# Down projection of a SwiGLU block by seven block products for eight, and four small changes of order

## The chip, the cores and the metric

The kernel runs on one core of a Trainium2 chip. The metric is the device time of one execution in microseconds (us); a time given for a kernel is the median of several executions. TensorE (PE) does the matmuls, VectorE (DVE), ScalarE (ACT) and GpSimd (POOL) the elementwise work, and SyncE (SP), ACT and POOL issue the transfers (DMAs).

## The reference

One decoder layer runs for a prompt of 512 tokens and for 8 samples of 8 tokens, 576 tokens T in all that share the weights. With D = 1024 and three residual blocks, each with an RMS norm before and after it:

```
x = x + post(Wout · [Mamba2-SSD heads, mLSTM heads](pre(x)))     # one input projection for both
x = x + post(CrossAttention(pre(x), memory keys and values))
x = x + post(Wdown · (silu(Wgate · pre(x)) * (Wup · pre(x))))    # SwiGLU
```

FFN_HIDDEN is 2816, which is 22 units of 128. All is float32, and the outputs are the tokens, the memory's keys and values and the new states of the recurrent heads.

## The kernel before

Features lie on the 128 partitions and tokens along the free dimension, so a weight tile of 128 x 128 is the loaded operand and a stretch of tokens is streamed. Float32 products are made from three matmuls in the type fp32r: each operand is split into a high part `hi` (a cast) and the rest `lo` (a subtraction), and hi·hi, hi·lo and lo·hi are summed in PSUM (helper `gemm`, L201 to L203). A weight unit is loaded by SP into `raw`, cast to `whi` by ACT (L181) and its low part `wlo` is made by DVE (L188), or by POOL with a DMA that adds the weight onto its negated high part (L185 and L186). Tokens are taken in halves of 256 and 320 (`HALVES`) or, in the last block, 288 and 288 (`E`).

In the SwiGLU block the gate and up products of hidden units 4 to 21 are computed by class `Pair`: for two units, two halves of the tokens and two halves of D it makes seven products of blocks instead of eight (a Strassen scheme in Winograd's form). A `Pair` loads two units (`raw`, `rawx`), forms sums and differences of weight blocks on DVE (`sums`, L1701 and L1702; `diffs`, L1709 and L1710), splits them again (`parts2`, `parts3`, `parts4`), and takes two low parts from POOL's adding DMAs (`low`, L1693 and L1694: ACT negates, the DMA adds; tiles `wacc` and half of `wlo`). Its products go through `mul` (L1742 to L1744), and `done` adds the parts that PSUM doesn't add by itself. The sums of the tokens' blocks are made once. A `Pair`'s `early` and `mid` and the last `Pair`'s `late` are interleaved, so that the next weights are prepared while the last are multiplied.

The gated values of a unit are split into `hh` and `hl`. The down projection takes the hidden units in three chunks of 8, 8 and 6 (`down_chunk`): for each of 8 output units and both token halves a plain `gemm` over the chunk, whose result is stored into (`ev_first`), and then added onto (`ev_add`, DVE L1831), the sum `f_ffn`. The third chunk ends in the last norm and the store of the tokens.

The order on each engine comes from the tile framework: instructions are issued in the order of the calls, unless `tc.issue_after(...)` ties one behind another; an engine runs its queue in order and waits at its head. A buffer with `bufs=2` or `3` is taken again when its last reader is done, and a PSUM bank in the same way.

Other places that the change touches: the first loads and casts (L299 to L312); the recurrent state's update `h` (POOL L725, PE `ps_hu` L728, DVE L729) beside the split of `wv`; the first mixer inputs `mixm_h` (ACT L1021) beside the copy `f_mix` (ACT L1015) that empties a PSUM bank; and the product `ps_xo` for output unit 3 of the cross-attention.

## Time and profile before

| what | value |
|---|---|
| median of 3 executions | 1112.0 us (1111.62 to 1112.33) |
| the profiled execution's own time | 1111.46 us |
| its span, first to last instruction | 1109.7 us |
| PE / DVE / ACT / POOL busy, share of the span | 99% / 64% / 53% / 19% |
| granted TensorE clock | 0.998 |
| chain that ended last: PE / DMA / DVE / ACT | 91% / 3% / 3% / 2% |

Shares are of the whole span; a matmul's own duration includes its pipeline, so the pace of PE is read from the starts of matmuls in a row, and lost time from the idle times before them. 1.8 us of the execution lie around the span.

### The profile page before, as it was taken

What the parts mean: (1) busy time and instruction counts of PE and PEld (TensorE: products, weight loads), DVE (VectorE), ACT (ScalarE), POOL (GpSimd) and SP (SyncE); (2) the same over time, 40 slices, a digit from 0 to 9 for tenths busy, and PEclk for the clock granted to TensorE, in tenths of its full rate; (3) what the DMA queues carried; (4) which work ended last, traced back from release to release, by engine and by line L of the source; (5) the groups of instructions that cost most, each with busy time, mean ns of one, the idle gap of its engine ahead of it and who ended that gap; (6) DMA issues with size and microseconds to landing.
All of it is one profiled execution on the core that took longest, in us unless ns stands there. A gap on an engine that the chain in (4) does not pass through costs nothing.

```text
span 1109.7 us, 21067 instructions
## 1 busy us (share of the span) xinstructions
PE 1095.9 (99%) x8424; PEld 1049.6 (95%) x8424; DVE 708.7 (64%) x1393; ACT 590.1 (53%) x1066; POOL 214.0 (19%) x289
## 2 busy tenths in 40 slices
PE   9999999999999999999999999999999999999997
PEld 8999888998999999999988889999999999999997
DVE  6996686558877774669554545776533665447555
ACT  6877523256654564647454445556434674246654
POOL 1443544213122111000244202101001110011000
PEclk9999999999999999999999999999999999999999
DMA  6775634334745358552567765735435674257532
GB/s 219 184 149 115 162 134 152 124 99 141 228 135 138 81 182 287 194 184 96 199 215 254 275 200 190 249 102 130 137 96 128 172 165 125 93 119 170 125 132 86
DMA packets 55078, 176.57 MB, mean 159 GB/s; under 512 B 6044, under 2 KB 10268, under 8 KB 54468
## 3 DMA queue, kind: packets, MB, share of 16 engines
q1 hardware_dynamic: 41156, 136.88, 37.0%
q0 software_dynamic: 13248, 37.23, 16.5%
q8 instruction: 66, 1.08, 0.4%
q10 hardware_dynamic: 576, 1.11, 0.3%
q14 instruction: 32, 0.26, 0.1%
HBM read 154.54 MB, written 20.65 MB: 158 GB/s over the span
## 4 chain that ended last, share of the span: by engine, by line
PE 91%; DMA 3%; DVE 3%; ACT 2%; issue 1%; SPq 0%; DVEq 0%; POOL 0%; POOLq 0%; ACTq 0%
PE ps_in L201 6%; PE ps_in L202 6%; PE ps_in L203 6%; PE ps_dn L201 4%; PE ps_dn L203 4%; PE ps_dn L202 4%; PE ps_o L201 3%; PE ps_o L203 3%; PE ps_o L202 3%; PE ps_g L1742 3%; PE ps_g L1743 3%; PE ps_g L1744 3%; PE ps_u L1742 3%; PE ps_u L1743 3%; PE ps_u L1744 3%; PE ps_v L777 2%
## 5 line engine op out<-in xcount | busy, mean ns | idle before, releaser
L181 ACT CAST whi<-raw 128x1024 fp32r<-128x1024 f32 x110 | 114.7, 1046 | 125.0 <-PE ps_in L202 28.6
L201 PE MATMUL ps_in<-uh,whi 128*128 128x320 f32 (+1 forms) x544 | 163.6, 301 | 0.0
L203 PE MATMUL ps_in<-uh,wlo 128*128 128x320 f32 (+1 forms) x544 | 163.3, 300 | 0.2 <-DVE wlo L188 0.2
L188 DVE TENSOR_TENSOR wlo<-raw,whi 128x1024 fp32r<-128x1024 f32 (+1 forms) x102 | 107.6, 1056 | 86.9 <-ACT whi L181 84.5
L202 PE MATMUL ps_in<-ul,whi 128*128 128x320 f32 (+1 forms) x544 | 162.6, 299 | 0.0
L201 PEld LDWEIGHTS ps_in<-uh,whi 128*128 128x128 f32 x544 | 103.1, 190 | 2.4 <-issue 1.7
L203 PEld LDWEIGHTS ps_in<-uh,wlo 128*128 128x128 f32 x544 | 103.0, 190 | 1.4 <-DVE wlo L188 0.4
L202 PEld LDWEIGHTS ps_in<-ul,whi 128*128 128x128 f32 x544 | 103.2, 190 | 0.6
L201 PE MATMUL ps_dn<-hh,whi 128*128 128x320 f32 (+1 forms) x280 | 82.6, 298 | 0.5 <-ACT whi L181 0.5
L203 PE MATMUL ps_dn<-hh,wlo 128*128 128x320 f32 (+1 forms) x280 | 81.9, 295 | 0.8 <-DVE wlo L188 0.8
L202 PE MATMUL ps_dn<-hl,whi 128*128 128x320 f32 (+1 forms) x280 | 82.1, 294 | 0.0
L203 PEld LDWEIGHTS ps_dn<-hh,wlo 128*128 128x128 f32 x280 | 52.7, 189 | 1.2 <-DVE wlo L188 1.2
L201 PEld LDWEIGHTS ps_dn<-hh,whi 128*128 128x128 f32 x280 | 52.2, 188 | 1.0 <-ACT whi L181 0.7
L202 PEld LDWEIGHTS ps_dn<-hl,whi 128*128 128x128 f32 x280 | 52.8, 188 | 0.0
L186 POOL DMA_DIRECT2D wlo<-win x32 | 27.8, 879 | 86.8 <-ACT wlo L185 78.6
L1742 PE MATMUL ps_u<-b,whi 128*128 128x288 f32 x144 | 42.5, 295 | 0.6 <-ACT ct L1774 0.6
L1743 PE MATMUL ps_u<-b,whi 128*128 128x288 f32 x144 | 42.5, 296 | 0.0
L1742 PE MATMUL ps_g<-b,whi 128*128 128x288 f32 x144 | 42.5, 295 | 0.0
L1743 PE MATMUL ps_g<-b,whi 128*128 128x288 f32 x144 | 42.5, 295 | 0.0
L1694 POOL DMA_DIRECT2D wacc<-wgate x9 | 7.8, 862 | 161.4 <-ACT wacc L1693 140.7
L201 PE MATMUL ps_o<-mixs_h,whi 128*128 128x320 f32 (+1 forms) x128 | 38.3, 299 | 0.5 <-ACT f_mix L1015 0.5
L203 PE MATMUL ps_xo<-qh,wlo 128*128 128x288 f32 x128 | 37.7, 296 | 0.7 <-DVE wlo L188 0.7
(728 smaller groups left out, 3665.2 us busy)
## 6 DMA issues: line engine op xcount, KB each, us to landing
raw<-win SPq DMA_DIRECT2D x35, 512.0 KB, 3.7
raw<-wout SPq DMA_DIRECT2D x17, 512.0 KB, 3.6
kva<-kc SPq DMA_DIRECT2D x16, 512.0 KB, 6.6
kva<-vc SPq DMA_DIRECT2D x16, 512.0 KB, 6.8
raw<-wdown SPq DMA_DIRECT2D x16, 512.0 KB, 3.6
raw<-wxq SPq DMA_DIRECT2D x13, 512.0 KB, 3.5
raw<-wgate SPq DMA_DIRECT2D x13, 512.0 KB, 3.7
raw<-wup SPq DMA_DIRECT2D x13, 512.0 KB, 4.9
```

The lines of the kernel that those rows point to most:

```text
L181: A.copy(hi[:, :n], raw[:, :n])
L186: G.dma_start(lo[:, a:b], src[:, a:b], accum_op=ALU.add)
L188: e.tensor_tensor(lo[:, a:b], raw[:, a:b], hi[:, a:b].bitcast(F32), op=ALU.subtract)
L201: mm(ps, wh, ah, start=i == 0, stop=False)
L202: mm(ps, wh, al, start=False, stop=False)
L203: m = mm(ps, wl, ah, start=False, stop=i == len(tiles) - 1)
L777: m = mm(o, ah, lo[:, j:j + 256], start=False, stop=k == KT - 1, skip_group_check=True)
L1694: G.dma_start(out, s.src[j, :, c], accum_op=ALU.add)
L1742: mm(ps, wh, b[0][:, k, :], start=start and k == 0, stop=False, skip_group_check=True)
L1743: mm(ps, wh, b[1][:, k, :], start=False, stop=False, skip_group_check=True)
L1744: m = mm(ps, wl, b[0][:, k, :], start=False, stop=k == 3, skip_group_check=True)
```

## The change

`Pair` becomes a base class `Seven` with two users: `Pair` for gate and up, and a new class `Down` for the down projection. The hidden units are now taken in four chunks: units 0 to 3 plainly, 4 to 9 and 10 to 15 by `Down`, and 16 to 21 plainly as before. A `Down` makes two output units for both token halves over six hidden units, three in each half of the inner dimension: 7 products of 3 blocks of three matmuls, 63 matmuls of 288 columns, where the plain way takes 72 of 256 and 320. Four `Down` make a chunk. Their weights are prepared as a `Pair`'s are, 768 columns wide instead of 1024, and their order in memory is changed on the host.

The products need sums of the hidden blocks. Class `Hidden` stores three of the four blocks of a pair of units (`put`) and makes four differences in place (`sums`, DVE) and one split, 1152 wide, where the fourth block had its split of 288. It takes more memory: a tile `te`, a longer slot for `u3h`, and a pool `rows` that is closed earlier and opened again as `rows2`. `run` interleaves `Pair`s and `Down`s: the gate pair 10, four `Down`, the up pair 10, pairs 12 and 14; then again from 16 with the next chunk. A `Pair`'s first negation (`wacc`) is tied behind the first cast `c1` of the step ahead (`behind`). The program has 984 matmuls for the down projection instead of 1056; those for gate and up stay.

The four small orders: `par`, a table of 150 columns, is loaded through POOL's queue instead of SP's, and the first cast of a weight is made by DVE; the split of the first `wv` weights comes behind the first addition onto `h`; the first three `mixm_h` come behind the last copy `htc` of `qk`; in `ps_xo` for unit 3 the matmuls with `wlo` of the first six blocks come behind the other matmuls of those (`late=6`).

```diff
-    def split(hi, lo, src, eng=None):
-        A.copy(hi, src)
+    def split(hi, lo, src, eng=None, cast=None):
+        (cast or A.copy)(hi, src)
...
             (wh, wl), ah, al = tiles[k], xh(k, t0, n), xl(k, t0, n)
             mm(ps, wh, ah, start=i == 0, stop=False)
             mm(ps, wh, al, start=False, stop=False)
-            m = mm(ps, wl, ah, start=False, stop=i == len(tiles) - 1)
+            for c in range(late) if i == late - 1 else [i] if i >= late else ():
+                m = mm(ps, tiles[order[c]][1], xh(order[c], t0, n), start=False, stop=c == len(tiles) - 1)
...
-    S.dma_start(par, I["par"])
+    G.dma_start(par, I["par"])
...
         if k % 2 == 0:
             S.dma_start(raws[1][:, c], I["win"][2][:, c])
-            split(wi[0][0][:, c], wi[0][1][:, c], raws[0][:, c])
+            split(wi[0][0][:, c], wi[0][1][:, c], raws[0][:, c], cast=V.tensor_copy if k == 0 else None)
         uhk = A.activation(uh[:, k, 0:T], xraw[:, k, :], AF.Copy, scale=PAR("g_pre", k))
         ulk = V.scalar_tensor_tensor(ul[:, k, :], xraw[:, k, :], PAR("g_pre", k), uh[:, k, 0:T].bitcast(F32),
                                      op0=ALU.mult, op1=ALU.subtract)
...
+    added = []
...
             for g in range(2):
                 ps = BP("ps_hu")
                 mm(ps, bm[:, g * P:(g + 1) * P], xst[:, g * 512:(g + 1) * 512], start=True, stop=True)
-                V.tensor_tensor(hn[:, 8 * g:8 * g + 8, :], hn[:, 8 * g:8 * g + 8, :],
-                                ps.rearrange("p (h k) -> p h k", h=8), op=ALU.add)
+                added.append(V.tensor_tensor(hn[:, 8 * g:8 * g + 8, :], hn[:, 8 * g:8 * g + 8, :],
+                                             ps.rearrange("p (h k) -> p h k", h=8), op=ALU.add))
...
     for h in range(4):
-        gemm_tok(I["wv"][h], U, UL, CHUNKS, v_evac(h), 1024)
+        with tc.issue_after(added[0].ins) if h == 0 else ExitStack():
+            units = [split_w(I["wv"][h][:, i, :], cut=1024) for i in range(2)]
+        gemm_tok(I["wv"][h], U, UL, CHUNKS, v_evac(h), units=units)
...
     for j in range(8):
         hm = qk[:, 4 * (j % 2) + j // 2, 0:TP]
-        with tc.issue_after(evs[0].ins) if j > 2 else ExitStack():
+        with tc.issue_after((evs[0] if j > 2 else htc).ins):
             A.activation(mixm_h[:, j, 0:TP], hm, AF.Copy, scale=ghalf[:, j:j + 1])
...
-            m = gemm(ps, [(*w, KT)], act(oh), act(ol), t0, n, k0, k1, [2, 3, 4, 5, 6, 7, 0, 1])
+            m = gemm(ps, [(*w, KT)], act(oh), act(ol), t0, n, k0, k1, [2, 3, 4, 5, 6, 7, 0, 1], 6 if j == 3 else 0)
...
+    class Seven:
+
+        behind = ()
+
+        def weights_of(s, src1, src2, side, low=(None, None)):
+            s.n, s.side, s.src1, s.src2, s.made = src1.shape[-1] // 2, side, src1, src2, low
+            s.LA, s.LB, s.all = slice(0, s.n), slice(s.n, 2 * s.n), slice(0, 2 * s.n)
             s.r1 = wp.tile([P, 1024], F32, name="raw", tag="raw", bufs=2)
-            S.dma_start(s.r1, s.src[j])
+            S.dma_start(s.r1[:, s.all], src1)
...
-            s.low(s.l1, s.r1, s.j)
-
-        def low(s, out, raw, j, c=slice(0, 1024)):
-
-            if ("gu"[s.up], j) in PRE:
-                G.dma_start(out, pre[:, PRE.index(("gu"[s.up], j)), c])
+            with ExitStack() as after:
+                for t_ in s.behind:
+                    after.enter_context(tc.issue_after(t_.ins))
+                s.low(s.l1[:, s.all], s.r1[:, s.all], s.src1, s.made[0])
+
+        def low(s, out, raw, src, made):
+
+            if made is not None:
+                G.dma_start(out, made)
             else:
                 A.activation(out, raw, AF.Copy, scale=-1.0)
...
+
             fh, fl = s.factor(w)
-            for k in range(4):
+            nk = s.n // P
+            for k in range(nk):
                 wh, wl = fh[:, k, :], fl[:, k, :]
-                mm(ps, wh, b[0][:, k, :], start=start and k == 0, stop=False, skip_group_check=True)
-                mm(ps, wh, b[1][:, k, :], start=False, stop=False, skip_group_check=True)
-                m = mm(ps, wl, b[0][:, k, :], start=False, stop=k == 3, skip_group_check=True)
+                mm(ps, wh, b[0][k], start=start and k == 0, stop=False, skip_group_check=True)
+                mm(ps, wh, b[1][k], start=False, stop=False, skip_group_check=True)
+                m = mm(ps, wl, b[0][k], start=False, stop=k == nk - 1, skip_group_check=True)
...
         def late(s):
-            s.mul(s.x, 5, parts(4), False)
+            s.mul(s.x, 5, tsum[4], False)
             s.done(1, 0, s.x)
             s.mul(s.z, 6, b22, False)
             s.done(0, 1, s.z, s.c2)
...
+            if s.then:
+                s.then()
+
+    class Hidden:
+
+        def __init__(s, hh, hl):
+            s.b = [t_.rearrange("p k (i t) -> p (k i) t", i=2) for t_ in (hh, hl)]
+            s.te = None
+
+        def rest(s):
...
+        def put(s, j, a, i, g):
+            if (a, i) != (0, 1):
+                split(*s.place((j - 4) // 2 % 3, {(0, 0): 4, (1, 0): 5, (1, 1): 6}[a, i]), g)
+
+        def sums(s, j):
+            q, g = (j - 4) // 2 % 3, gates(j)
+            for out, p, m in ((g[0][0], g[0][1], g[0][0]), (g[0][1], g[1][1], g[0][1]), (g[1][1], g[1][1], g[0][0]),
+                              (g[1][0], g[1][0], g[1][1])):
+                V.tensor_tensor(out, p, m, op=ALU.subtract)
+            hi, lo = [t_[:, (8, 0)[q]:(8, 0)[q] + 4, :] for t_ in s.b] if q < 2 else [s.rest()[:, 0:4, :], s.rest()[:, 4:8, :]]
+            split(hi, lo, gt[:, 4 * (j // 2 % 2):4 * (j // 2 % 2) + 4, :])
+
+        def block(s, m):
+            return [[s.place(q, m)[e] for q in range(3)] for e in range(2)]
+
+    class Down(Seven):
+
+        def __init__(s, j, k0, hid):
+            s.j, s.hid, s.name = j, hid, "dn"
+            s.weights_of(I["wdown"][j, :, k0:k0 + 768], I["wdown"][j + 1, :, k0:k0 + 768], 1 - j // 2 % 2)
+
+        def add(s, a, i, ps):
+            o = f2[:, s.j + a, E[i]]
+            V.tensor_tensor(o, o, ps, op=ALU.add)
+
+        def early(s):
+            s.x, s.z, y = s.bank(), s.bank(), s.bank()
+            s.mul(s.x, 0, s.hid.block(4))
+            s.add(0, 0, s.x)
+            s.mul(y, 1, s.hid.block(5))
+            s.add(0, 0, y)
+            s.mul(s.z, 3, s.hid.block(0))
+            s.add(1, 1, s.z)
+            s.mul(s.x, 2, s.hid.block(3), False)
+            s.add(0, 1, s.x)
+
+        def mid(s):
+            s.mul(s.x, 4, s.hid.block(1), False)
+            s.add(1, 1, s.x)
+
+        def late(s):
+            s.mul(s.x, 5, s.hid.block(2), False)
+            s.add(1, 0, s.x)
+            s.mul(s.z, 6, s.hid.block(6), False)
+            s.add(0, 1, s.z)
+
+    def run(make, last):
+
+        for m in make:
+            p = m()
+
+            if seq:
+                p.behind = [seq[-1].c1] if isinstance(p, Pair) else []
+            seq.append(p)
+            p.prepare()
+            p.early()
+            if last:
+                last.late()
+            p.mid()
+            last = p
...
+    def w_first(j):
+        with tc.issue_after(pp[0].ev3.ins) if j < 2 else ExitStack():
+            return weights(("d", j), I["wdown"][j, :, 0:512], 512, cut=512)
+
+    down_chunk(4, [(j, i) for j in range(8) for i in (1, 0)], pp[1], w_first, ev_first, 4)
+    seq.extend(pp)
+    last = run([pair(j, up, stores[0]) for j in (6, 8) for up in range(2)], None)
+
+    def downs(k0, store):
+        return [lambda j=j: Down(j, k0, store) for j in (0, 2, 4, 6)]
+
...
+    for n_, j0 in enumerate((10, 16)):
+        store = stores[-1]
+        last = run([lambda: Pair(j0, 0, None)] + downs(512 + 768 * n_, store), last)
+        stores.append((Plain if n_ else Hidden)(SL0("hh%d" % n_), SL(2, "hl%d" % n_, F32R)))
+        last = run([pair(j0, 1, stores[-1])] + [pair(j, up, stores[-1]) for j in (j0 + 2, j0 + 4) for up in range(2)], last)
```

On ACT, at the start of the program (`uh`: scaled tokens, `mcol`: a column made from `par`; DMAHW stands for a transfer of SP's or ACT's queue, DMASW for one of POOL's), there stood

```order
L307 DMA xraw_87<-xT 128x576 x2
L391 ACT_TABLE_LOAD
L391 ACTIVATE mcol_433<-par_77 128x1 [waits DMAHW1_49]
L311 ACTIVATE uh_88<-xraw_87,par_77 128x576 [waits DMAHW0_49]
L192 CAST whi_120<-raw_124 128x256 [waits DMAHW2_49]
L311 ACTIVATE uh_88<-xraw_87,par_77 128x576 [waits DMAHW3_49]
```

and now stands

```order
L309 DMA xraw_87<-xT 128x576 x2
L313 ACT_TABLE_LOAD [waits DMAHW0_49]
L313 ACTIVATE uh_88<-xraw_87,par_77 128x576 [waits DMASW0_49]
L393 ACTIVATE mcol_433<-par_77 128x1
L192 CAST whi_122<-raw_125 128x256 [waits DMAHW2_49]
L313 ACTIVATE uh_88<-xraw_87,par_77 128x576 [waits DMAHW3_49]
```

The activation table's load, which waited for nothing, now waits for the first tokens, and `uh` stands ahead of `mcol`.

On DVE, within the plain down projection of the second chunk (`wlo`: low part of a down weight, `sw`, `rawx`, `raw`: weights of the next pair), there stood

```order
L1831 TENSOR_TENSOR f_ffn_9204<-f_ffn_9204,ps_dn_11168 128x256 [waits PE_49]
L188 TENSOR_TENSOR wlo_11314<-raw_11311,whi_11313 128x1024 [waits DMAHW1_49,Activation_49]
L1831 TENSOR_TENSOR f_ffn_9204<-f_ffn_9204,ps_dn_11194 128x320 [waits PE_49]
L1702 TENSOR_TENSOR sw_8841<-sw_8841,raw_11428 128x512 [waits DMAHW3_49]
L1709 TENSOR_TENSOR rawx_11430<-raw_11428,rawx_11430 128x512
L1831 TENSOR_TENSOR f_ffn_9204<-f_ffn_9204,ps_dn_11226 128x256 [waits PE_49]
L188 TENSOR_TENSOR wlo_11372<-raw_11369,whi_11371 128x1024 [waits DMAHW2_49,Activation_49]
L1831 TENSOR_TENSOR f_ffn_9204<-f_ffn_9204,ps_dn_11252 128x320 [waits PE_49]
L1831 TENSOR_TENSOR f_ffn_9204<-f_ffn_9204,ps_dn_11284 128x256 [waits PE_49]
```

and at the entry into the first four `Down` now stands (`te`: sums of hidden blocks, `gt`: gated values; `ps_dn`: products of the down projection)

```order
L1778 TENSOR_TENSOR gt_8840<-ps_g_10096,ct_7805 128x288 [waits PE_49]
L193 TENSOR_TENSOR te_9991<-gt_8840,te_9991 128x1152 [waits Activation_49]
L193 TENSOR_TENSOR wlo_10237<-raw_10229,u3h_7798 128x384 [waits DMASW7_49,Activation_49]
L1858 TENSOR_TENSOR f_ffn_9208<-f_ffn_9208,ps_dn_10254 128x288 [waits PE_49]
L1858 TENSOR_TENSOR f_ffn_9208<-f_ffn_9208,ps_dn_10150 128x288 [waits PE_49]
L1858 TENSOR_TENSOR f_ffn_9208<-f_ffn_9208,ps_dn_10256 128x288 [waits DVE_49]
L1858 TENSOR_TENSOR f_ffn_9208<-f_ffn_9208,ps_dn_10149 128x288 [waits PE_49]
L193 TENSOR_TENSOR wlo_10245<-sw_8841,whi_10244 128x768 [waits Activation_49]
L1733 TENSOR_TENSOR u3l_7799<-rawx_10231,whi_10236 128x3x128 [waits Activation_49]
L1858 TENSOR_TENSOR f_ffn_9208<-f_ffn_9208,ps_dn_10150 128x288 [waits DVE_49,PE_49]
```

Between two additions onto `f_ffn` there was one operation on weights or two; now the 1152-wide split of the hidden sums and a part of the weights stand ahead of four additions in a row.

On DVE, where the samples' states `h` are updated (`lm`, `qk`, `xs`, `ec`: work of the recurrent heads), there stood

```order
L448 SCALAR_TENSOR_TENSOR qk_443<-ps_in_2292,rxb_91 128x320 [waits PE_49]
L188 TENSOR_TENSOR wlo_2451<-raw_2448,whi_2450 128x1024 [waits DMAHW7_49,DMASW5_49,Activation_49]
L729 TENSOR_TENSOR h0_1892<-h0_1892,ps_hu_1903 128x512 [waits Pool_49]
L631 SCALAR_TENSOR_TENSOR xs_90<-xs_90,par_77,ps_yi_1432 128x512 [waits PE_49]
L630 TENSOR_TENSOR ec_1462<-ec_1462,ps_yn_1464 128x384 [waits PE_49,Activation_49]
L729 TENSOR_TENSOR h0_1892<-h0_1892,ps_hu_1906 128x512 [waits PE_49]
```

and now stands

```order
L450 SCALAR_TENSOR_TENSOR qk_443<-ps_in_2292,rxb_91 128x320 [waits PE_49]
L732 TENSOR_TENSOR h0_1892<-h0_1892,ps_hu_1903 128x512 [waits Pool_49]
L188 TENSOR_TENSOR wlo_2451<-raw_2448,whi_2450 128x1024 [waits DMAHW6_49,DMASW6_49,Activation_49]
L633 SCALAR_TENSOR_TENSOR xs_90<-xs_90,par_77,ps_yi_1432 128x512 [waits PE_49]
L632 TENSOR_TENSOR ec_1462<-ec_1462,ps_yn_1464 128x384 [waits PE_49,Activation_49]
L732 TENSOR_TENSOR h0_1892<-h0_1892,ps_hu_1906 128x512 [waits PE_49]
```

The first addition onto `h0` has moved ahead of the low part `wlo` of a weight.

More of the change, by code (lines that the diff above doesn't have):

```diff
@@ L1731, in prepare @@
+            return K3(t_[0][:, c]), s.ls if w == 4 else K3(t_[1][:, s.LA if w == 5 else c])
         def prepare(s):
@@ new lines, in run, with pair, make @@
+    def run(make, last):
[10 more added lines that the diff above has]
+            last = p
+        return last
+    def pair(j, up, store):
+        def make():
+            with tc.issue_after(pp[1].ev2.ins) if j == 6 and not up else ExitStack():
+                return Pair(j, up, store.put, (lambda: store.sums(j)) if up and isinstance(store, Hidden) else None)
+        return make
```

144 lines of the change are left out of this document (77 added, 67 removed).

## The prediction

> **What bounds the kernel now.** I read the page's busy shares and chain of waits first, then the list of PE's waits, then busy time by stretches, and last the groups of instructions and the timeline at the places that the change touches.
>
> ```profile
> span 1109.7 us, 21067 instructions
> PE 1095.9 (99%) x8424; PEld 1049.6 (95%) x8424; DVE 708.7 (64%) x1393; ACT 590.1 (53%) x1066; POOL 214.0 (19%) x289
> PE 91%; DMA 3%; DVE 3%; ACT 2%; issue 1%; SPq 0%; DVEq 0%; POOL 0%; POOLq 0%; ACTq 0%
> ...
> PE ps_hu L728 <- DVE h L729: 1.1, 1, 1.1
> PE ps_dn L203 <- DVE wlo L188: 0.8, 2, 0.6
> PE ps_in L325 <- ACT whi L192: 0.8, 1, 0.8
> PE ps_xo L203 <- DVE wlo L188: 0.7, 1, 0.7
> PE ps_u L1742 <- ACT ct L1774: 0.6, 1, 0.6
> PE ps_dn L201 <- ACT whi L181: 0.5, 1, 0.5
> PE ps_o L201 <- ACT f_mix L1015: 0.5, 1, 0.5
> ```
>
> PE is busy 99% of the span and 91% of the chain. The list of what PE waited for (us in total, times, longest) is short: each entry is a single wait of about a microsecond or less. So two things can shorten this kernel, fewer matmuls and the removal of these single waits, and any wait that PE gets anew adds to the time in full. What a matmul costs is read from stretches (length, then busy time and number of instructions of each engine):
>
> ```profile
> 850.70:934.80 84.10, 84.10 (x639) 84.10 (x638) 54.57 (x96) 57.62 (x95) 11.10 (x13) 1.00 0.64 154
> 934.80:991.40 56.60, 55.99 (x422) 55.79 (x421) 24.45 (x39) 13.78 (x18) 2.56 (x3) 1.00 0.39 108
> ```
>
> The first is gate and up of units 8 to 15, 288 columns each: 84.10 / 639 = 0.1316 us a matmul without a gap, at a granted clock of 1.00. The second is the plain down projection of the second chunk: 56.60 / 422 = 0.134 us, its start included.
>
> **The change, part by part.**
>
> *Fewer matmuls.* 1056 - 984 = 72 fall away on the engine that sets the time: 72 x 0.1316 = 9.5 us, or 9.7 by the second row. I take -9.5.
>
> [...]
>
> *The new down steps.* A `Down` keeps PE for 63 x 0.1316 = 8.3 us. The other engines must keep up, so their work is priced by groups of the stretch from 850 to 990 (count, busy us, mean ns):
>
> ```profile
> L188 DVE TENSOR_TENSOR wlo<-raw,whi 128x1024 fp32r<-128x1024 f32 x8 | 9.8, 1222 | 4.5 <-ACT whi L181 4.5
> L193 DVE TENSOR_TENSOR hl<-gt,hh 128x288 fp32r<-128x288 f32 x16 | 7.2, 456 | 7.6 <-ACT hh L192 7.6
> L1701 DVE TENSOR_TENSOR sw<-rawx 128x512 f32<-128x512 f32 x8 | 5.5, 688 | 0.1
> L1693 ACT ACTIVATE wacc<-raw 128x1024 fp32r<-128x1024 f32 x8 | 8.5, 1060 | 15.4 <-DMA raw<-wup 9.9 <-DMA raw<-wgate 5.5
> L1698 ACT CAST whi<-raw 128x1024 fp32r<-128x1024 f32 x8 | 8.3, 1044 | 3.8 <-PE ps_g L1743 3.5 <-PE ps_u L1743 0.3
> L192 ACT CAST u3h<-raw 128x512 fp32r<-128x512 f32 x8 | 5.0, 619 | 1.5 <-PE ps_g L1743 0.7 <-PE ps_u L1743 0.6 <-DVE raw L1710 0.2
> L1753 ACT ACTIVATE gt<-ps_g 128x288 f32<-128x288 f32 x4 | 1.6, 398 | 0.0
> L1694 POOL DMA_DIRECT2D wacc<-wup x4 | 3.4, 848 | 31.2 <-ACT wacc L1693 24.1 <-ACT cc L1778 7.1
> ```
>
> Between these widths I go in a straight line: on DVE 384 columns cost 0.56 us, 768 cost 0.96 and 1152 cost 1.36; on ACT 768 cost 0.83 and 1152 cost 1.15. A `Down` has on DVE six operations of 384, one of 768 and seven additions of 288: 6 x 0.56 + 0.96 + 7 x 0.456 = 7.5 us of the 8.3. If a narrow operation costs as much as the next wider row, it is 6 x 0.688 + 1.222 + 7 x 0.456 = 8.5, which is 0.2 us too much. ACT has two negations, three casts of 768 and one of 384, some 4.4 us. So DVE has little room, and each addition that is late holds a bank that PE wants again.
>
> The tightest place that I find is the entry, since the 1152-wide split of the hidden sums comes there too (rows of order quoted with the change). With zero at the first matmul of the `Down` at the head of that piece: ACT's cast of its first weight waits for a buffer that a matmul 14 places ahead frees. That matmul starts 14 x 0.132 = 1.85 us before zero and runs about 0.4 (two rows of single matmuls below); the cast takes 0.83, the silu behind it 0.40 and the 1152-wide cast 1.15: it ends near +1.0. DVE's part of that split takes 1.36, to +2.4; PE wants it 20 matmuls in, at +2.6. The weight's low part and two additions follow, 0.56 + 0.46 + 0.46, to +3.4 and +3.9, and PE wants these banks 26 and 28 matmuls in, at +3.4 and +3.7. So PE stalls about 0.2 us, and the additions behind are in time. I take 0.3 at each of the two entries and 0.15 at the other six `Down`: +1.5. Bounds: 0, if all is in time, and 4, if each `Down` is 0.2 over and each entry loses 1 us more.
>
> *Starts of chunks.* Of PE's waits on down weights (0.8 in two, 0.5 in one), the 0.6 at the start of the second chunk goes with that chunk. At the start of the first, the weights come 512 wide instead of 1024, so cast and subtraction take 0.62 and 0.69 us instead of 1.05 and 1.22; I take half of the 0.7 there. Together -0.9, bounds 0 and -1.3.
>
> *Sums of hidden blocks.* For each pair of units DVE makes four differences of 288 more, and a split of 1152 instead of 288: 4 x 0.456 + 1.36 - 0.46 = 2.7 us, in a time in which gate and up take PE 168 x 0.1316 = 22.1 us. DVE's load there goes from 54.57 / 84.10 = 65% to 77%. It is hidden by DVE's idle third, cost 0; without that cover six such pairs would cost 16 us. The order `behind` gives the negation more time and costs ACT nothing.
>
> *First pair behind the first chunk.* That chunk is half as long, so its weights' negation and adding transfer have less time. A lateness of 0.2 us is what I take, bounds 0 and 0.7:
>
> ```profile
> wacc<-wup POOLq DMA_DIRECT2D x9, 512.0 KB, 5.7
> raw<-wdown SPq DMA_DIRECT2D x4, 384.0 KB, 3.0
> xraw<-xT ACTq DMA_DIRECT2D x2, 288.0 KB, 3.2
> ```
>
> *Order at `h`.* The timeline (start, length) shows why PE waited there:
>
> ```profile
> 144.73 9.50 POOL L725 TENSOR_TENSOR h<-h,vt 128x1024 f32<-128x1024 f32 x4 [2.60 <-PE ps_hs L718]
> 149.89 2.55 DVE L188 TENSOR_TENSOR wlo<-raw,whi 128x1024 fp32r<-128x1024 f32 x1
> 152.36 0.68 DVE L729 TENSOR_TENSOR h<-h,ps_hu 128x512 f32<-128x512 f32 x1
> 153.18 0.47 PE L728 MATMUL ps_hu<-stb,bm 96*128 96x512 f32 x1 [1.08 <-DVE h L729]
> ```
>
> A `wlo` that takes 1.22 elsewhere took 2.55 while POOL worked, and the addition stood behind it. Ahead of it, the addition ends near 150.6, before PE asks: -1.1. The addition kept its 0.68 beside POOL. `wlo` then starts 0.7 later, still beside POOL, and feeds a product several microseconds on. Bounds -1.2 and 0.
>
> *Order at `mixm_h` and `ps_xo`.*
>
> ```profile
> 395.29 0.37 ACT L1015 COPY f_mix<-ps_o 128x256 f32<-128x256 f32 x1
> 395.72 0.41 PE L201 MATMUL ps_o<-mixs_h,whi 128*128 128x320 f32 x1 [0.46 <-ACT f_mix L1015]
> 654.82 1.23 DVE L188 TENSOR_TENSOR wlo<-raw,whi 128x1024 fp32r<-128x1024 f32 x1 [1.73 <-PE ps_ots L1347]
> 656.10 0.40 PE L203 MATMUL ps_xo<-qh,wlo 128*128 128x288 f32 x1 [0.73 <-DVE wlo L188]
> ```
>
> In `ps_xo` twelve matmuls, 1.6 us, now come before the first with `wlo`, more than the 1.23 that it takes: -0.7. At 395 the three `mixm_h` no longer stand ahead of the two copies of `qk`, and the work behind these on DVE ends earlier, so a bank is free: -0.5. For both the bounds are 0 and these values.
>
> *The start.*
>
> ```profile
> 1.65 1.28 ACT L391 ACT_TABLE_LOAD   x1 [1.65 <-PEq L2107]
> 4.12 0.20 ACT L391 ACTIVATE mcol<-par 128x1 f32<-128x1 f32 x1 [1.18 <-DMA par<-par]
> 4.22 0.76 ACT L311 ACTIVATE uh<-xraw,par 128x576 fp32r<-128x576 f32 x1
> 5.02 0.82 DVE L312 SCALAR_TENSOR_TENSOR ul<-xraw,par,uh 128x576 fp32r<-128x576 f32 x1 [0.51 <-ACT uh L311]
> 5.66 0.54 PE L325 MATMUL ps_in<-uh,whi 128*128 128x256 f32 x2 [0.82 <-ACT whi L192]
> ```
>
> The first weights are asked for 0.45 us earlier, since `par` leaves SP's queue, and their cast needs no ACT. But the table's load, which now ends at 2.93 while ACT waits for `par`, will wait for the tokens, which land near 0.74 + 3.2 = 3.9. It then ends at 5.2, `uh` at 6.0 and `ul` at 6.8. PE starts near 6.0 instead of 5.66, and again waits some tenths for `ul`: +0.5. Bounds: -0.45, if the load doesn't wait, and +1.2, if `par` comes late through POOL's queue too.
>
> **Sum**, against the profiled execution of 1111.46 us: -9.5 + 1.5 - 0.9 + 0.2 - 1.1 - 0.5 - 0.7 + 0.5 = -10.5, which gives 1101.0. The median before, 1112.0, is 0.5 above its profiled execution, so I forecast 1101.5 us. All bounds at their good ends give 1098, all at their bad ends 1108.
>
> **Rivals.**
>
> *DVE paces the down steps.* For it: 7.5 of 8.3 us, and DVE waits at the head of its queue for ACT's casts. Against: the walk above finds only tenths. If a `Down` takes 9.3 us, 1 us more than its matmuls, eight cost 8 instead of 1.5: 1108. It decides when operations of 384 columns cost over 0.69 us, or waits on ACT fill what is left.
>
> *The waits of the small orders move on* instead of going: all three come back a few instructions later, as queues this full allow. Against: each has a product behind it that needs nothing else. Then 2.3 us fewer go: 1104.
>
> *The adding transfers come late, and it gets slower.* Place: the third matmul of each `Down`, which needs `wacc`. From the negation on it is 0.84 + 0.85 + 5.7 = 7.4 us. The weight's own load can start only when the step two ahead is split, some 3 us into that step; with 0.33 + 3.0 us of loading, `wacc` lands near 13.7 of 16.6 us, 2.9 ahead. It decides when a transfer takes over 8.6 us; at 10.7 each of eight steps loses 2.1 us, 17 in all: 1117. Against: the 5.7 were measured with DMA engines at 64%, and a `Down` moves less than a `Pair`.
>
> That the change doesn't do what it says is excluded: the 984 matmuls are in the program.
>
> **How the numbers follow.** My sum gets 0.66, with its own range 1098 to 1105; the waits that move on 0.12; DVE's pace 0.15; late transfers 0.07. Under 2.2 us, 0.2%, this kernel can't be told from no change. Faster: the sum, the moved waits and most of DVE's pace, 0.87; within 0.2%, the upper part of DVE's pace, 0.06; slower 0.07. The range is 1097.5 to 1108.5: it takes in the first two cases and about half of the third.
>
> **What would show it.** Right: 72 fewer matmuls at 0.132 us with PE gap-free through most of the eight steps; waits `ps_hu` on `h` and `ps_xo` on `wlo` gone; the table's load near 3.9 us and PE's first weight product near 6.0; PE's waits on `f_ffn` and `te` under 2 us in all. Wrong: DVE over 95% in the down steps with `ps_dn` waiting for `f_ffn` at every step (DVE's pace), `ps_dn` waiting for the DMA of `wacc` (late transfers), or the small waits under other names.

## The result and the profile after

The changed kernel took 1101.69 us (median; 1098.65 to 1104.22), the kernel before, on the same chip, 1112.01: a ratio of 0.9901 [0.9891, 0.9912], or 11.0 us less [9.8 to 12.1] by the ratio (the medians differ by 10.3). The forecast was 1101.5. The runs of the changed kernel differ by 5.6 us where those of the kernel before differ by 1.2, and the profiled execution, 1104.22 us, is the longest of them. It lies 2.5 us above the median, so it shows waits that shorter executions have less of.

The page of the changed kernel (span; busy time, share of the span and instructions; the chain that ended last):

```profile
span 1102.4 us, 21188 instructions
PE 1088.5 (99%) x8352; PEld 1041.7 (94%) x8352; DVE 752.9 (68%) x1506; ACT 612.4 (56%) x1105; POOL 231.8 (21%) x306
...
PE 86%; DMA 6%; issue 4%; DVE 2%; ACT 1%; POOL 0%; DVEq 0%; SPq 0%; POOLq 0%; ACTq 0%
```

The 72 matmuls are gone (8424 before), and PE is still busy 99% of the span. DMA's part of the chain went from 3% to 6%, but that share doesn't follow the time: with the four small orders alone, slower than before, it is 2%, and with the Down projection alone, faster, 2% too. The list of what PE waited for (us in total, times, longest) says more:

```profile
PE ps_in L327 <- ACT uh L313: 1.3, 1, 1.3
PE ps_ss L1495 <- DVE ssqxo L1571: 1.1, 1, 1.1
...
PE ps_sa L1322 <- DMA kva<-kc: 0.9, 2, 0.7
...
PE ps_u L1761 <- DMA wacc<-wup: 0.8, 1, 0.8
PE ps_ss L1495 <- DVE ssqxo L269: 0.8, 1, 0.8
PE ps_dn L1759 <- ACT whi L1713: 0.5, 1, 0.5
PE ps_u L1759 <- ACT whi L192: 0.4, 1, 0.4
PE ps_xo L205 <- DVE wlo L188: 0.2, 1, 0.2
```

Of the waits that I had quoted of before, these have left the list: `ps_hu` on `h`, `ps_o` on `f_mix`, `ps_u` on `ct`, the down weights of the old chunks, and of `ps_xo` 0.5 of the 0.7. But others are new or longer: the start (1.3, was 0.8), `ps_ss` on `ssqxo` (0.8 and 1.1, was 0.2 once), `kva` (0.9, was 0.2), and an adding transfer and two casts of weights (0.8, 0.4 and 0.5). Behind one of them the clock fell. Here are the stretches around 702 us, of before and then of after (length, busy time and number of instructions of PE, PEld, DVE, ACT, POOL, granted clock, DMA share, GB/s):

```profile
700.00:704.00 4.00, 3.82 (x30) 3.59 (x29) 2.95 (x8) 3.17 (x8) 0.86 (x2) 1.00 0.55 196
704.00:708.00 4.00, 4.00 (x33) 4.00 (x33) 1.84 (x5) 0.40 (x1) 1.35 (x3) 1.00 0.68 205
```

```profile
700.00:704.00 4.00, 2.90 (x24) 2.67 (x22) 2.20 (x6) 2.89 (x7) 0.00 (x0) 1.00 0.76 286
704.00:708.00 4.00, 4.00 (x21) 4.00 (x21) 1.23 (x6) 1.27 (x2) 2.05 (x3) 0.60 0.33 83
708.00:712.00 4.00, 4.00 (x32) 4.00 (x31) 2.41 (x4) 1.24 (x3) 0.00 (x0) 0.97 0.60 209
```

Behind the wait of 1.1 us the granted clock was 0.60 over 4 us. PE is "busy" for all of them and starts 21 matmuls, not 33: at 0.13 us each some 1.6 us more on top of the 1.1. A busy share of 100% says nothing of this; the count and the clock do.

### The profile page after: what moved, and what is told of

The parts are those of the page before. It is cut to its first block, busy times and chain, and to the rows that moved or that the text cites. A ratio compares the mean times of both kernels' runs of the same rounds, so it can differ in the third digit from the quotient of the medians.

```text
span 1102.4 us, 21188 instructions
## 1 busy us (share of the span) xinstructions
PE 1088.5 (99%) x8352; PEld 1041.7 (94%) x8352; DVE 752.9 (68%) x1506; ACT 612.4 (56%) x1105; POOL 231.8 (21%) x306
## 3 DMA queue, kind: packets, MB, share of 16 engines
q8 instruction: 65, 1.06, 0.4%
## 4 chain that ended last, share of the span: by engine, by line
PE 86%; DMA 6%; issue 4%; DVE 2%; ACT 1%; POOL 0%; DVEq 0%; SPq 0%; POOLq 0%; ACTq 0%
PE ps_in L202 7%; PE ps_in L203 7%; PE ps_in L205 6%; PE ps_o L202 3%; PE ps_o L205 3%; PE ps_o L203 3%; PE ps_u L1761 3%; PE ps_u L1759 3%; PE ps_u L1760 3%; PE ps_g L1759 3%; PE ps_g L1761 3%; PE ps_g L1760 3%; PE ps_v L780 2%; PE ps_v L779 2%; PE ps_v L778 2%
## 5 line engine op out<-in xcount | busy, mean ns | idle before, releaser
L181 ACT CAST whi<-raw 128x1024 fp32r<-128x1024 f32 (+1 forms) x102 | 103.2, 1015 | 93.5 <-PE ps_in L203 28.7
L188 DVE TENSOR_TENSOR wlo<-raw,whi 128x512 fp32r<-128x512 f32 (+1 forms) x94 | 92.9, 989 | 67.3 <-ACT whi L181 64.4
L1708 ACT ACTIVATE wacc<-raw 128x1024 fp32r<-128x1024 f32 (+1 forms) x26 | 25.7, 992 | 26.9 <-DMA raw<-wdown 16.2
L1732 ACT CAST whi<-rawx 128x1024 fp32r<-128x1024 f32 (+1 forms) x26 | 25.7, 989 | 25.9 <-PE ps_dn L1760 15.2
L202 PE MATMUL ps_xo<-qh,whi 128*128 128x288 f32 x128 | 38.2, 300 | 0.0
L202 PE MATMUL ps_xq<-u2h,whi 128*128 128x320 f32 (+1 forms) x128 | 38.2, 302 | 0.0
L205 PE MATMUL ps_o<-mixm_h,wlo 128*128 128x256 f32 (+1 forms) x128 | 38.1, 298 | 0.0
L203 PE MATMUL ps_xq<-u2l,whi 128*128 128x320 f32 (+1 forms) x128 | 38.0, 298 | 0.0
L203 PE MATMUL ps_o<-mixm_l,whi 128*128 128x256 f32 (+1 forms) x128 | 38.0, 297 | 0.0
L205 PE MATMUL ps_xq<-u2h,wlo 128*128 128x320 f32 (+1 forms) x128 | 37.9, 296 | 0.0
```

The source lines that it names most:

```text
L181: A.copy(hi[:, :n], raw[:, :n])
L188: e.tensor_tensor(lo[:, a:b], raw[:, a:b], hi[:, a:b].bitcast(F32), op=ALU.subtract)
L202: mm(ps, wh, ah, start=i == 0, stop=False)
L203: mm(ps, wh, al, start=False, stop=False)
L205: m = mm(ps, tiles[order[c]][1], xh(order[c], t0, n), start=False, stop=c == len(tiles) - 1)
L1708: A.activation(out, raw, AF.Copy, scale=-1.0)
```

## The experiments

Times of experiments are medians, and ratios are against the kernel before on the same chip. A difference from the kernel before in us is worked out from the ratio; one between two experiments on the same chip is that of the medians, and one across chips that of the ratios.

**The parts apart.** Four kernels: the four small orders alone on the kernel before; the Down projection alone (`behind` included); the change without the order at the start; the change without the order in `ps_xo`. In the code the last two are

```diff
-    G.dma_start(par, I["par"])
+    S.dma_start(par, I["par"])
...
-            split(wi[0][0][:, c], wi[0][1][:, c], raws[0][:, c], cast=V.tensor_copy if k == 0 else None)
+            split(wi[0][0][:, c], wi[0][1][:, c], raws[0][:, c])
```

```diff
-            m = gemm(..., [2, 3, 4, 5, 6, 7, 0, 1], 6 if j == 3 else 0)
+            m = gemm(..., [2, 3, 4, 5, 6, 7, 0, 1], 0)
```

The four small orders alone. Expected:

> The kernel before with the four small orders alone (start, h, mixm_h, ps_xo), without any Down. Theory A, the sum on record: -1.1 (h) - 0.5 (mixm_h) - 0.7 (ps_xo) + 0.5 (start) = -1.8 us, a ratio near 0.998. Theory B, from the trace of the changed kernel: the start loses more (PE's first weight product at 6.8 instead of 5.66) and what ps_xo gains comes back as a wait of ps_ss near 672, so the two orders at h and mixm_h (-1.2 and -0.6) are just paid for the start: 0 to -0.8 us.

Measured: 1113.6 us, 1.0017 [1.0007, 1.0026]: 1.9 us slower [0.8 to 2.9], where I had forecast 1.8 faster. Neither theory had a loss.

The Down projection alone. Expected:

> The changed kernel with the four small orders undone, Down alone. Theory A, the sum on record: -9.5 + 1.5 - 0.9 + 0.2 = -8.7 us, a ratio of 0.992. Theory B: Down alone carries the whole gain and the small orders nothing, then -9.5 to -10.5 us, a ratio of 0.991, the same as the whole change. If DVE paced the down steps it would be -3 us.

Measured: 1100.26 us, 0.9897 [0.9881, 0.9914]: 11.5 us less [9.6 to 13.2], where the sum had 8.7: B, at its upper end or above.

Without the order at the start. Expected:

> The changed kernel with only the start undone: par on SP's queue, the first cast on ACT, so the activation table's load waits for nothing. Theory A: the start cost about 1 us (first weight product at 6.8 instead of 5.66), which goes through to the end: 1 us below the changed kernel, a ratio to before of 0.989. Rival: the microsecond is lost again in later waits for transfers (ps_ss near 672 and 702), and the time is that of the changed kernel.

Measured: 1099.34 us, 0.9884 [0.9869, 0.9899]: 12.9 us less than before, which fits A; the interval overlaps that of the change, so its rival isn't excluded.

Without the order in `ps_xo`. Expected:

> The changed kernel with late=6 taken back: ps_xo of unit 3 in the old order. Theory A: the wait of 0.7 us on wlo near 655 is back and the time is 0.7 us above the changed kernel. Rival: the wait near 655 is back, but the wait of ps_ss on ssqxo near 672 (0.8 us) goes in its place, since ACT there waits for a weight from memory, and the time is the same.

Measured: 1100.35 us, 0.9897 [0.9881, 0.9914]: 11.5 us less than before, much as the change (11.0). The trace is the rival's: the wait of 0.7 us on `wlo` is back, and that of `ps_ss` on `ssqxo` L269 (0.8) is gone. By the time alone A's 0.7 us isn't excluded.

So the forecast's total was right and its split was not: Down gives all of the gain, and the four small orders together cost time on the kernel before and gain nothing beside Down. The Down projection alone against before, stretch from 752 to 1050 us (first before, then Down alone):

```profile
752.00:1050.00 298.00, 296.03 (x2227) 294.90 (x2226) 161.50 (x273) 154.90 (x255) 28.13 (x33) 1.00 0.54 135
```

```profile
752.00:1050.00 298.00, 297.90 (x2243) 297.15 (x2241) 212.64 (x393) 181.47 (x306) 42.22 (x50) 1.00 0.66 153
```

PE has 0.1 us of idle time there instead of 2.0, although DVE went from 161.50 to 212.64 us (54% to 71%) and ACT from 154.90 to 181.47. The waits of before in this stretch (0.8, 0.6 and 0.5, quoted with the prediction) have no successor at all in this run.

**Without both orders that seemed to cost.** Expected:

> The change without the order at the start and without the order in ps_xo; the down projection with seven products, the order at h and the order at mixm_h stay. Theory A (the two orders cost time each, and independently): without the start alone the time was 0.9884 of before, without ps_xo's order alone 0.9897, with all 0.9901; so the two gains of about 1.9 us and 0.4 us add up, and the time is about 0.988 of before, near 1098.5 us. Theory B (the order in ps_xo is worth its 0.88 us, and the 0.4 us were spread between runs): 0.7 us more than without the start alone, near 1100. In the trace both expect the wait of 0.88 us near 655 us back, and the table's load near 1.7 us.

Measured: 1099.09 us, 0.9887 [0.9871, 0.9904], 12.6 us less. That is neither better nor worse than without the start's alone; theory A's sum of the two (0.988) lies within the interval, and so does B.

**Which half of the start's order costs.** The change with `par` on SP's queue, the first cast still on DVE. Expected:

> The change with par on SP's queue again, as before; the cast of the first weights stays on DVE. Theory A (the load of the table waits for the tokens, and this alone makes uh late): par lands near 4.1 us instead of 5.96, but the table's load still runs from about 4.6 to 5.9 and uh starts near 5.95; PE's first weight product stays near 6.8 and the time at that of the change, within 0.5 us. Theory B (par through POOL's queue makes uh late, and the table's load would be in time): uh starts near 4.7 and the time is 1 to 2 us less than that of the change, as with both undone.

Measured: 1099.77 us, 0.9887 [0.9873, 0.9902]. My theory A fell; the numbers of B (`uh` near 4.7, 1 to 2 us less than the change) came out. The timeline (start, length) of ACT's first instructions, with DVE's `ghalf`, which needs `par` alone, and PE's first product, first of the change, then with `par` back on SP's queue:

```profile
4.64 1.28 ACT L313 ACT_TABLE_LOAD   x1 [4.64 <-DMA xraw<-xT]
...
5.99 0.78 ACT L313 ACTIVATE uh<-xraw,par 128x576 fp32r<-128x576 f32 x1
5.99 0.17 DVE L376 TENSOR_SCALAR ghalf<-par 128x8 f32<-128x8 f32 x1 [0.83 <-DMA par<-par]
...
6.67 0.19 ACT L393 ACTIVATE mcol<-par 128x1 f32<-128x1 f32 x1
...
6.82 0.92 PE L327 MATMUL ps_in<-uh,whi 128*128 128x256 f32 x4 [1.34 <-ACT uh L313]
```

```profile
1.67 1.28 ACT L393 ACT_TABLE_LOAD   x1 [1.67 <-PEq L2234]
...
3.86 0.20 ACT L393 ACTIVATE mcol<-par 128x1 f32<-128x1 f32 x1 [0.91 <-DMA par<-par]
...
4.49 0.77 ACT L313 ACTIVATE uh<-xraw,par 128x576 fp32r<-128x576 f32 x1 [0.42 <-DMA xraw<-xT]
...
5.57 0.50 PE L327 MATMUL ps_in<-uh,whi 128*128 128x256 f32 x2 [0.37 <-DVE whi L192]
```

With `par` on SP's queue ACT's first activation is `mcol`, and the table's load in front of it (line 393) runs while ACT has nothing to do. With `par` on POOL's queue `mcol` stands behind `uh`, the load belongs to `uh` (line 313) and starts only when the tokens are there. But `uh` needs `par` too, and that landed later as well: `ghalf` starts at 5.99 us, in the same moment as `uh` and 0.07 us after the table's load. It is the same in the three other profiles with `par` on POOL's queue (`uh` and `ghalf` at 5.98, 6.16 and 6.27, the load's end at 5.94, 6.11 and 6.20). So the load behind the tokens and the later `par` each hold `uh` to the same time, and this run, which takes both back, can't tell one from the other; a run with an early load and a late `par` was not made.

Nor is the cast on DVE free: with `par` back on SP's queue PE waits 0.6 us for `ul`, which DVE makes behind that cast and its low part. The first product of the first `ps_ss`, some 150 matmuls on, starts at 25.12 us in the change, at 24.94 with `par` back, and at 24.10 with the cast back too. So PE's early start comes from the move of `par` back; what of the time is due to `par` and what to the cast is not shown, as the intervals of all three kernels overlap.

**How much room DVE has in a Down.** The two sums of 384 columns are computed once more in each of the eight steps, or three times more, into the same place, in the version without both orders:

```diff
         def sums(s):
             V.tensor_tensor(sw[:, s.LB], s.r2[:, s.LA], s.r2[:, s.LB], op=ALU.add)
             V.tensor_tensor(sw[:, s.LA], sw[:, s.LB], s.r1[:, s.LA], op=ALU.subtract)
+            for _ in range(1 if isinstance(s, Down) else 0):
+                V.tensor_tensor(sw[:, s.LB], s.r2[:, s.LA], s.r2[:, s.LB], op=ALU.add)
+                V.tensor_tensor(sw[:, s.LA], sw[:, s.LB], s.r1[:, s.LA], op=ALU.subtract)
```

Once more. Expected:

> As without start's and ps_xo's orders, and in each of the eight Down steps the two sums of 384 columns are computed once more (the same values into the same place): 2 x 0.553 = 1.1 us of DVE more per step, 8.9 us in all. DVE then has 7.4 + 1.1 = 8.5 us in a step that keeps PE 63 x 0.1316 = 8.3 us. Theory A (DVE did not set the pace, it had 0.9 us to spare in a step): at most 0.2 us are missing per step, which the pairs around take up, and the time grows by 0 to 2 us. Theory B (DVE or what it waits for paces the down steps already): nearly all of the 8.9 us appear, at least 6.

Measured: 1099.29 us, 0.9884 [0.9869, 0.9898], 0.2 us from the 1099.09 without the repeat, as A had it. Three times more. Expected:

> As the run with the sums once more, but three times more: 6 x 0.553 = 3.3 us of DVE more per step, 10.7 us in a step that keeps PE 8.3 us. Theory A (0.9 us of DVE to spare in a step, and DVE is the bound beyond it): 2.4 us per step are missing, 19.6 us in eight; what DVE has to spare in the pairs ahead of and behind each row of four steps takes 1 to 2 us of it per row, so 15 to 19 us more. Theory B (DVE paces already): 26 us more. A rise below 12 would say that DVE had far more room than its busy time in a step tells.

Measured: 1113.43 us, 1.0007 [0.9996, 1.0019], 14.3 us more than without the repeats: all of the gain is gone. Of the 26.5 us of DVE that were added 12.2 were hidden, 1.5 per step; A had counted 0.9 in a step and 1 to 2 per row of four, and lies just above the measured value, B far off. What PE waited for from 750 to 1050 us there:

```profile
PE ps_g L1764 <- DMA wacc<-wgate: 4.3, 2, 2.2
PE ps_dn L1762 <- DVE f_ffn L1861: 2.0, 3, 0.9
PE ps_dn L1763 <- DVE te L193: 1.2, 2, 0.8
```

The additions into `f_ffn` and the split of the hidden sums (`te`) come late, as the rival on DVE's pace had it. The adding transfers of the first pair behind each row of Down come late too, 4.3 us in all, much as the third rival had it; that a late DVE frees the raw weights' buffers late is what I take to be behind it, but it was not tried apart.

**Two, one and one of the small orders on the kernel before.** The orders at `h` and at `mixm_h` alone. Expected:

> The kernel before with two of the four small orders alone: the first weights of wv behind the first addition to h, and the first mixm_h behind the copy of the last qk. Theory A (both waits go for good): 1.24 us at 151.8 and 0.62 us at 395.0 are gone, 1.7 to 1.9 us less than before, ratio near 0.9984. Theory B (they only move on): the same waits come back within some 10 us under other names, less than 0.5 us won.

Measured: 1110.39 us, 0.9983 [0.9974, 0.9992]: 1.9 us less, A again. From 140 to 400 us PE's list of waits is empty in that run. The order at the start alone. Expected:

> The kernel before with the order at the start alone: par on POOL's queue, the first cast on DVE. Theory A (par, planned late on POOL's queue, puts the activation of mcol behind uh, so that the table's load stands behind the wait for the tokens): the load runs from about 4.6 to 5.9 instead of 1.65 to 2.93, uh starts near 6.0 and PE's first product near 6.8; 1.1 to 1.4 us more than before, and up to 2.7 if the granted clock falls in the first 20 us as it did with all four small orders. Theory B (the time that the four small orders cost lies elsewhere): within 0.4 us of before.

Measured: 1114.09 us, 1.0015 [1.0006, 1.0024]: 1.7 us more, as A had it. The order in `ps_xo` alone. Expected:

> The kernel before with the order in ps_xo alone: six low products late for j = 3. Theory A (the wait moves on: the stretch up to ps_ss ends with a chain through ACT, whose casts wait for the weights to be loaded, and not with PE's count of products): the 0.89 us near 655 go, 0.3 to 0.6 come near 661 and 0.8 to 1.0 at ps_ss, and the time is that of before or up to 0.6 us more. Theory B (as forecast): 0.7 us less than before. With the other two runs of this batch the parts should add up to the 1.9 us that all four small orders cost together: -1.8 + 1.3 to 2.7 + 0.3 gives -0.2 to +1.2, so that 0.7 to 2 us would stay open.

Measured: 1112.66 us, 1.0001 [0.9993, 1.001]: no change, which is A too. The waits of PE from 630 to 700 us with it, and then the last steps of ACT and DVE ahead of `ps_ss`, first before, then with the order:

```profile
PE ps_ss L1491 <- DVE ssqxo L269: 0.8, 1, 0.8
PE ps_xo L205 <- DVE wlo L188: 0.2, 1, 0.2
```

```profile
671.25 1.05 ACT L1468 CAST w<-raw 128x1024 fp32r<-128x1024 f32 x1 [1.43 <-DMA raw<-wup]
672.43 0.41 ACT L266 ACTIVATE sq<-ps_xo 128x288 f32<-128x288 f32 x1
...
672.88 0.46 DVE L267 TENSOR_TENSOR ssqxo<-ssqxo,sq 128x288 f32<-128x288 f32 x1 [2.96 <-ACT sq L266]
```

```profile
671.38 1.05 ACT L1471 CAST w<-raw 128x1024 fp32r<-128x1024 f32 x1 [2.00 <-DMA raw<-wup]
672.43 0.41 ACT L268 ACTIVATE sq<-ps_xo 128x288 f32<-128x288 f32 x1
...
672.87 0.46 DVE L269 TENSOR_TENSOR ssqxo<-ssqxo,sq 128x288 f32<-128x288 f32 x1 [3.39 <-ACT sq L268]
```

Of PE's 0.7 at `ps_xo` 0.5 are won, PE comes to `ps_ss` that much earlier, and waits 0.8 there: the last square needs ACT, ACT is held at a cast by the load of `wup`, and this chain ends at the same time (672.88 and 672.87) in both. In the kernel before PE arrived just with it, so no row of PE's waits showed it.

The three parts add up to -1.9 + 1.7 + 0.1 = -0.1 us; all four orders together cost 1.9 [0.8 to 2.9]. Each of the three carries an interval of 1 us to either side, so the 2 us between could just be the measurement; but the profile of the four orders has 1.2 us of waits at 663 and 674 us (the two of `ps_xo`'s order) and 1.2 us for `kva` between 551 and 587, where the kernel before has 0.7 at 655 and 0.2 for `kva`; and the clock fell at its start (0.63 from 8.5 to 12.5 us), which cost more than with a clock of 1.00 (see the next section). Whether these grow because the orders are combined, or from run to run, is open.

**Without the tie of the negations.** The version without both orders, and the negation of a gate or up weight no longer behind the cast of the step ahead:

```diff
-                p.behind = [seq[-1].c1] if isinstance(p, Pair) else []
+                p.behind = []
```

Expected:

> As without start's and ps_xo's orders, and without the tie that puts the negation of a gate or up weight behind the cast of the step ahead. ACT and DVE then take their steps of the pairs in another order, and PE some of its own. Theory A (ACT has room: 56% busy; the tie only decides which of two ready instructions is first): within 1 us of the same kernel with the tie, ratio near 0.9885. Theory B (a negation of 1.06 us that goes first delays a cast that PE waits for, once per pair): waits of PE on whi of 0.3 to 1 us in the pairs, 3 to 8 us more, ratio 0.991 to 0.996.

Measured: 1109.07 us, 0.9965 [0.9952, 0.9979]: 8.7 us more than with the tie (0.9887), an estimate from the two ratios, whose intervals make it 6 to 11: at the upper end of B or above it, and A is out. PE's waits from 750 to 1050 us, where the version with the tie has none, then ACT at 892 and at 814 us, and the clock behind the two longest:

```profile
PE ps_g L1759 <- ACT whi L1713: 5.4, 2, 2.8
PE ps_g L1759 <- ACT cc L1803: 1.8, 1, 1.8
```

```profile
892.72 1.05 ACT L1732 CAST whi<-rawx 128x1024 fp32r<-128x1024 f32 x1 [1.10 <-PE ps_u L1760]
897.33 1.06 ACT L1708 ACTIVATE wacc<-raw 128x1024 fp32r<-128x1024 f32 x1 [3.56 <-DMA raw<-wup]
898.29 0.41 ACT L192 CAST hh<-gt 128x288 fp32r<-128x288 f32 x1
898.62 1.04 ACT L1713 CAST whi<-raw 128x1024 fp32r<-128x1024 f32 x1
```

```profile
814.19 1.06 ACT L1708 ACTIVATE wacc<-raw 128x1024 fp32r<-128x1024 f32 x1 [4.01 <-DMA raw<-wup]
815.15 0.38 ACT L1803 COPY cc<-ps_g 128x288 f32<-128x288 f32 x1
```

```profile
899.60:903.60 4.00, 3.89 (x19) 3.89 (x20) 2.84 (x4) 2.74 (x6) 0.85 (x1) 0.61 0.82 133
...
1005.30:1009.30 4.00, 4.00 (x20) 4.00 (x21) 2.93 (x4) 2.61 (x5) 0.85 (x1) 0.63 0.86 140
```

The negation waits 3.56 us at the head of ACT's queue for `wup`, which lands late behind a row of Down; the cast of the weight that PE needs next stands behind it. It happens once per row, 2.6 and 2.8 us, and each time the clock falls to about 0.6: 19 and 20 matmuls in 4 us are 11 or 12 fewer than elsewhere (31), 1.5 us. The 1.8 us are the same behind the first, plain chunk, where the negation waits 4.01 us for `wup` and the copy `cc` stands behind it. So what costs is the negation's wait for its load, at three places, and not its own 1.06 us in every pair, as B had it. 5.4 + 1.8 + 0.2 of waits and 2 x 1.5 make 10.4, and the two profiled spans differ by as much (1107.2 and 1096.8); PE's other waits are 0.8 us shorter in the run without the tie, so the account closes to about a microsecond.

## Why the prediction was right, and where its steps were wrong

The total was right to 0.2 us; of its terms about half were, and the errors cancelled. That it came so near is luck: the interval of the measured gain is 2.3 us wide, and three terms were off by 0.8 to 2.6 us each.

*Fewer matmuls, -9.5: right.* 8352 for 8424, at the same spacing: 297.90 / 2243 = 0.133 us a matmul in the stretch with Down, and 296.03 / 2227 = 0.133 before.

*New Down steps, +1.5, and starts of chunks, -0.9: the sum of the two should have been about -2.* That is the 11.5 us of Down alone less the 9.5 [-0.1 to -3.7 by its interval], and the 1.9 us of PE's idle time that went in the stretch above say the same. The prices were right: groups of the run with Down alone, against 0.56, 0.96 and 0.456 forecast,

```profile
L1853 DVE TENSOR_TENSOR f_ffn<-f_ffn,ps_dn 128x288 f32<-128x288 f32 x56 | 24.7, 450 | 6.9 <-PE ps_dn L1756 6.2
...
L193 DVE TENSOR_TENSOR wlo<-sw,whi 128x768 fp32r<-128x768 f32 x8 | 7.6, 955 | 0.5 <-ACT whi L192 0.5
...
L1720 DVE TENSOR_TENSOR raw<-raw,sw 128x384 f32<-128x384 f32 x8 | 4.5, 559 | 4.2 <-ACT whi L1708 4.2
```

so a Down has 6 x 0.555 + 0.955 + 7 x 0.45 = 7.4 us on DVE, where the forecast had 7.5. The failing step is "I take 0.3 at each of the two entries and 0.15 at the other six": in the run with Down alone the entries cost nothing, and 1.1 us per step could be added to DVE without a sign of it in the time. In the profiled execution of the change one entry does show (`ps_dn` on `whi`, 0.5). And "together -0.9" left out the wait of `ps_u` on `ct` (0.6), which went as well in that run and in the change (in three other profiles with Down 0.3 to 0.6 of it are there), and half of one that went whole.

*Hidden sums at 0, and `behind` "costs ACT nothing": right in size, but the reason for the tie was missed.* I read it as more time for the negation. It decides which of two instructions waits at the head of ACT's queue, and without it 8.7 us of the gain would not be there. It was part of the forecast's total all along, but unpriced: the walk through ACT's queue at the end of a row of Down was not made.

*First pair and `wacc`, +0.2: it differs from run to run.* In the profiled execution of the change an adding transfer at 810 us cost PE 0.8, and `whi` behind it 0.4; without the order in `ps_xo` 0.2 of it showed, with Down alone and without the start's order none. The third rival had feared the transfers of Down itself; those land sooner than a `Pair`'s (the change's profile; weights, queue, KB each, median us from issue to landing):

```profile
wacc<-wup POOLq DMA_DIRECT2D x9, 512.0 KB, 5.5
...
wacc<-wdown POOLq DMA_DIRECT2D x8, 384.0 KB, 4.7
```

*Orders at `h` and `mixm_h`, -1.1 and -0.5: right.* 1.9 us by the run with these two alone, both waits gone for good.

*Order in `ps_xo`, -0.7: wrong, 0.1.* The second rival, that waits move on, was right here and only here: the stretch was bound by a chain through the load of `wup`, ACT and `ssqxo`, and a wait of PE inside it was not on the path.

*The start, +0.5: wrong, 1.7 [0.7 to 2.7].* "The table's load ... will wait for the tokens" came out, but later than forecast. The failing steps are two landings. The tokens, "which land near 0.74 + 3.2 = 3.9", let the load start at 4.64. And `par`, which the sum took to be in time, landed at 1.28 + 4.7 = 5.98. So `uh`, which was to end at 6.0, ran from 5.99 to 6.77, and PE started at 6.82 instead of "near 6.0", 1.2 us later than in the kernel before. That is the bad end of the term's own bounds, "+1.2, if `par` comes late through POOL's queue too", in its condition and in its size. The rest is the clock, which the forecast did not have: with the start's order alone, PE's first wait was 1.7 us, and behind it

```profile
8.50:12.50 4.00, 4.00 (x23) 4.00 (x23) 4.00 (x9) 4.00 (x9) 0.00 (x0) 0.68 1.06 378
```

23 matmuls were started, where the profiled execution of the change, with a wait of 1.3 us, has 32 and a clock of 1.00. What is left of it shows at the first product of the first `ps_ss`: it starts at 23.95 to 24.71 us (24.15 in the middle) in the nine profiles that have nothing of the start's order, at 25.12 and 25.41 in the two that have it and a clock of 1.00, and at 26.64 and 26.82 in the two in which the clock fell too (the start alone, the four small orders). So the start costs 1.0 to 1.3 us, and 2.5 to 2.7 when the clock falls.

Together, by the runs of the parts: -11.5 - 1.9 + 1.7 + 0.1 = -11.6, against -11.0 measured and -10.5 in the forecast's sum. The kernels with Down and with `par` on SP's queue came to between 1099.09 and 1100.26 us, the change itself to 1101.69; the intervals of their ratios overlap, so that a version faster than the change is likely but not shown.

## What to carry to other kernels

Here 0.5 us of PE's wait at `ps_xo` went and the time changed by 0.1, since the chain that ended the stretch ran elsewhere: find the last thing that the stretch waits for, and follow it back through the other engines and their loads, before you credit the wait. Ask of every instruction that waits for a transfer what stands behind it on its engine; here a negation on ACT waited 3.56 us for `wup` ahead of a ready cast, and one line that puts the cast first was worth 8.7 us. And when a transfer moves to another queue, look at when it lands there (`par` took 4.7 us on POOL's queue, 3.3 on SP's) and at which instruction becomes the first on the engine that uses it: what came with that instruction, here a table's load, moved with it, from 1.65 to 4.64 us.

## What the runs showed of the hardware

*A wait of PE can cost twice.* Waits of 1.1 us (702 us, the change), 1.7 us (the start, with its order alone and with the four small orders) and 2.6 and 2.8 us (without the tie) were followed by 3.41 us at a granted clock of 0.50 (in the change from 704.84 to 708.25 us), which rows of 4 us show as 0.60 to 0.68, some 1.5 us more each. Others as long were not, and the clock behind them was 1.00: 1.1 us at 151.8 us in the kernel before, 1.3 us at the start of the change, 1.8 us at 813 us without the tie and 2.1 and 2.2 us at 902 and 1009 us with the sums three times more. So the length of a wait alone does not decide.

Nor does the time for which PE was busy around it. The 3.41 us with the wait at 702 us in the change and the 3.41 us behind them:

```profile
701.43:704.84 3.41, 2.31 (x19) 2.08 (x18) 2.91 (x8) 2.68 (x8) 0.18 (x1) 1.00 0.58 220
704.84:708.25 3.41, 3.41 (x16) 3.41 (x15) 0.51 (x4) 0.43 (x1) 1.87 (x3) 0.50 0.38 92
```

The same wait with the sums three times more, and in that run 3.41 us with most of the 2.2 us at 1009:

```profile
698.79:702.20 3.41, 2.27 (x19) 2.04 (x17) 1.96 (x5) 2.77 (x6) 0.00 (x0) 1.00 0.60 189
702.20:705.61 3.41, 3.41 (x28) 3.41 (x29) 1.48 (x7) 1.38 (x2) 2.06 (x3) 1.00 0.36 95
...
1009.40:1012.81 3.41, 1.62 (x12) 1.63 (x13) 2.69 (x5) 1.07 (x2) 0.50 (x1) 1.00 1.04 187
```

In the 3.41 us ahead of the four other falls PE was busy for 0.84 to 1.68 us. But in the 3.41 us with the wait of `ps_ss` PE was busy for 2.31 and 2.27 us in the two runs above, and the clock fell only in the change; and with 1.62 us at 1009 it stayed at 1.00. What decides is open. The changed kernel's spread of 5.6 us is open too: the granted clock of its six executions lies between 0.997 and 0.999, an estimate of 2 us, and does not order them (1100.78 us at 0.997, 1104.22 at 0.998).

*`par` landed later through POOL's queue.* The table, 75 KB, took 4.7 us from issue to landing there and was issued at 1.28 us; through SP's queue, in the kernel before, it took 3.3. In the three other profiles with POOL's queue it took 4.7 to 5.0.
